# A hybrid attention block in split precision: halves of outputs summed by one VectorE reduction, MLP high parts squared by ScalarE

## The chip, the cores and the metric

The kernel runs on one core of one Trainium2 chip. The metric is the device time of one execution in microseconds (us); less is better.

## The reference, cut to what matters

Two layers of a transformer block on 512 tokens `x` and 256 context tokens `z` with width 1024. Each layer projects the tokens, runs three mixers beside each other (retention, neighbourhood attention, latent attention), merges them, and ends with a squared-ReLU MLP. In layer 1 the context is no longer carried on. All arithmetic is float32.

```python
def attend_blocks(q, k, v):
    ...
        s = jnp.einsum('bhqd,bhkd->bhqk', qi, k).astype(jnp.float32)
        p = jax.nn.softmax(s, axis=-1).astype(v.dtype)
        return jnp.einsum('bhqk,bhkv->bhqv', p, v)
def retention_chunkwise(q, k, v, log_gamma, s0):
    ...
    scores = jnp.einsum('bhncd,bhnsd->bhncs', qc, kc) * decay_mat[None, :, None]
    inner = jnp.einsum('bhncs,bhnsv->bhncv', scores, vc)
    kv_chunk = jnp.einsum('bhnsd,bhnsv->nbhdv', kc * k_decay[None, :, None, :, None], vc)
    ...
    cross = jnp.einsum('bhncd,nbhdv->bhncv', qc * q_decay[None, :, None, :, None], s_prev)
def sq_relu_mlp(h, p):
    return jnp.square(jax.nn.relu(h @ p['w_ff1'])) @ p['w_ff2']
```

## The kernel before

**Split precision.** TensorE multiplies in a rounded format (F32R). So that nothing is lost, each operand is kept as a pair: a high part, which ScalarE makes by copying the value into the rounded type (`hi_of`, the copy is at L381), and a low part, the value less its high part, which VectorE makes (`lo_of`, the subtraction at L384, on GpSimd for a few tiles). `split_into` calls both. A product of two pairs takes three passes (`mm3`): high with high (L428 or L643), high with low (L429, L644), low with high (L430, L645). Weights come from memory in tiles of 128x1024 (`wraw`) and are split in the same way into `wsp`.

**Halves.** In the attention's second product, values times probabilities, the value operand holds its high parts and its low parts side by side, 128 columns each. So an output bank holds two halves for every 256 columns, and their sum is the result. `gather_o` (L613 to L619) makes that sum for the neighbourhood and the latent attention: ScalarE copies one half out of the bank into a scratch tile `go` (L618), VectorE adds the other half from the bank (L619). It is called 80 times, on 512 columns each time. `Retention.prep` does the same for the chunks' key-value sums (L1292, L1293; 12 times), `Retention.item` in its step `s1` for its outputs `ro` (L1376, L1377; 40 times). Behind the sum of `s1` come the group norm's statistics, a power on GpSimd (L1386), and the gating. The retention's masked scores `pf` get their low part from GpSimd.

**Retention's preparation.** Behind the key-value sums, `prep` folds the chunk states (L1301), splits them into `st`, scales the queries into `qc` (L1319) and splits these into `op`; GpSimd casts copies of high parts (L665) and low parts (L666, the low part behind the high one).

**The MLP.** Eight blocks of 512 hidden columns, j = 0 to 7. For each, four weight tiles of the first matrix make four groups of hidden columns (i = 0 to 3): TensorE fills a bank, ScalarE applies Relu out of it into the scratch tile `rl` (L1751), VectorE squares `rl` in place (L1752), and the result is split into the operand `hid` (L381, L384). Then four weight tiles of the second matrix use these operands; the three first hidden groups are multiplied ahead, the fourth last. Blocks 1 to 6 handle all tokens in one round (512 columns of `x` and, in layer 0, 256 of `z`), blocks 0 and 7 go through the tokens in rounds of 256 columns. That makes 104 tiles `rl`, 56 with 512 columns and 48 with 256.

**Order.** The program is written stage by stage; the framework's scheduler arranges the instructions within each engine's queue, and each engine then works through its queue in order, waiting by semaphores for what the head of the queue needs. A few early loads are pinned to their written order. Memory for tiles comes from pools: 13 buffers of 128x512 (`sgl`, to which `go`, `rl`, `ro`, `qc` belong), 30 of 128x1024 (`dbl`), 3 of `wsp`. TensorE's banks: three for dense products (`pd`), two for the retention's and transposed products (`pst`), one for the attention outputs that gather_o empties (`pso`). An output bank is free again when the last of its readers is done.

Of the kernel before, what the change touches and what calls it, by code (L numbers as in the profile page):

```python
# [12 lines left out]
ALU = mybir.AluOpType  # L13
# [297 lines left out]
def block_kernel(ctx, tc, xT, zT, cond, wu, sp, bias, tab, out):  # L311
# [27 lines left out]
    def sgl(s="s"):  # L339
        return sgls.tile([128, 512], F32, tag="sgl", name=nm(s))  # L340
# [272 lines left out]

    def gather_o(t, o, nblk):

        v = o[:, : 256 * nblk].rearrange("p (b q) -> p b q", q=256)
        tmp = sgl("go")[:, : 128 * nblk].rearrange("p (b q) -> p b q", q=128)
        act.activation(tmp, v[:, :, 128:256], AF.Copy)  # L618
        dve.tensor_tensor(t, v[:, :, 0:128], tmp, op=ALU.add)  # L619

    def fold(y, t, odd):

# [528 lines left out]
    class Retention:  # L1151
# [39 lines left out]
        def prep(self, p2):  # L1191
# [89 lines left out]
            for c in range(3):  # L1281
                ps = bank_d()
                for o in range(2):
                    dst = ps[:, 256 * o : 256 * o + 256]
                    for i in range(2):
                        t = kt[2 * c + i]
                        v = R(vs[2 * c + i][:, 256 * o : 256 * o + 256])
                        pe.matmul(dst, R(t[:, 128 * o : 128 * o + 128]), v, start=i == 0, stop=False)
                        pe.matmul(dst, R(t[:, 256 + 128 * o : 256 + 128 * o + 128]), v, start=False, stop=i == 1)
                pv = ps.rearrange("p (h t v) -> p h t v", h=2, t=2)  # L1290
                s = kvt[c].rearrange("p (h v) -> p h v", h=2)
                act.activation(s, pv[:, :, 0], AF.Copy)  # L1292
                dve.tensor_tensor(s, pv[:, :, 1], s, op=ALU.add)  # L1293
                kvs.append(s)
                yield cost(8 * 256)

# [31 lines left out]
        def item(self, p2, o, c):  # L1328
# [25 lines left out]
            def s1():  # L1354
# [18 lines left out]
                            pe.matmul(ops[dr][:, ct], R(a), R(b), start=n == 0, stop=n == len(mms) - 1)  # L1373
                ov = st["ov"] = sgl("ro").rearrange("p (c t v) -> p c t v", c=2, t=2)
                for dr in range(2):
                    act.activation(ov[:, :, dr], ops[dr][:, :, 0], AF.Copy)  # L1376
                    dve.tensor_tensor(ov[:, :, dr], ops[dr][:, :, 1], ov[:, :, dr], op=ALU.add)  # L1377

                mv = small.tile([128, 4, 2], F32, tag="mv", name=nm("mv"))
                st6 = small.tile([128, 4, 6], F32, tag="st6", name=nm("st6"))  # L1380
# [240 lines left out]
    for l in range(DEPTH):  # L1621
# [119 lines left out]
        for j in range(8):  # L1741
            apart = j in (0, 7)
            for rnd in [[r] for r in rounds] if apart else [[(b, slice(0, n)) for b, (_, n) in enumerate(bufs)]]:
# [3 lines left out]
                for i in range(4):  # L1747
                    w = weight(l, "ff1", j, i)
                    for g, ps in enumerate(fm_groups(w, 0, hs, KT)):
                        t = sgl("rl")[:, : ns[g]]  # L1750
                        act.activation(t, ps, AF.Relu)  # L1751
                        dve.tensor_tensor(t, t, t, op=ALU.mult)  # L1752
                        split_into(hid[g][i], t)
                    later.step(0.0 if apart else ADA_MLP)
                    pend.step()
                last = j == 7
# [108 lines left out]
```

## Time and profile before

| | |
|---|---|
| time, median of 3 runs | 2628.12 us (2626.32 to 2634.21) |
| the profiled execution's own time | 2628.3 us |
| its span (first to last instruction) | 2626.5 us |
| mean granted clock of TensorE | 0.98 of full speed |
| TensorE busy (matmuls) | 2515.5 us, 96% of the span, 15218 instructions |
| VectorE busy | 1782.5 us, 68%, 3434 instructions |
| ScalarE busy | 1155.7 us, 44%, 2176 instructions |
| GpSimd busy | 333.4 us, 13%, 321 instructions |
| DMA | 329.43 MB moved, mean 125 GB/s |

A profile comes from one execution. PE is TensorE's matmul row, PEld its weight loads, DVE is VectorE, ACT ScalarE, POOL GpSimd; L619 is line 619 of the kernel. An instruction is written as engine, line, operation, tile written `<-` tiles read, size; a busy time is the sum over the instructions, and behind a bar stands how long the engine had stood idle before them and whose end it waited for. PEclk is the share of full clock that TensorE was granted.

### The profile page before, as it was taken

Reading aid. Unit: us, or ns where it says so; the run is one execution under the profiler, and the core shown is the slowest. Engines: PE = TensorE matmul, PEld = TensorE weight load, DVE = VectorE, ACT = ScalarE, POOL = GpSimd, SP = SyncE. Lnnn points to the kernel's source line nnn. Section 1 sums busy time; section 2 is a strip of 40 time slices with the busy share of each in tenths; the row PEclk is TensorE's granted clock in tenths of the full one; section 3 lists DMA queues with packets and bytes.
Section 4 is the critical chain, followed back from the end, with each engine's and each line's share of the span. In section 5 each row is a group of like instructions: output and inputs, shape, how many; then the busy total and the mean of one; then the engine's idle time right before and its main releaser. Section 6 shows DMA issues by size and latency. Waiting matters only on the chain. (4 is left out here: it accounts for less than half of the span.)

```text
span 2626.5 us, 39849 instructions
## 1 busy us (share of the span) xinstructions
PE 2515.5 (96%) x15218; PEld 2234.2 (85%) x15218; DVE 1782.5 (68%) x3434; ACT 1155.7 (44%) x2176; POOL 333.4 (13%) x321
## 2 busy tenths in 40 slices
PE   6999999998999998999999999999999899999997
PEld 4899998987888877888888878889888788988887
DVE  8566556777878886667556767665668768744457
ACT  4555545564333345322222446554555434732325
POOL 6201102234202000000000000010214310000000
PEclk7999999999999999999999999999999999999998
DMA  6222223423565633444444424323343356433333
GB/s 241 80 82 81 70 81 110 128 79 112 200 229 169 200 120 103 125 131 137 125 132 137 136 83 138 98 82 105 109 145 99 113 192 193 137 105 96 97 97 121
DMA packets 142995, 329.43 MB, mean 125 GB/s; under 512 B 16978, under 2 KB 54738, under 8 KB 142804
## 3 DMA queue, kind: packets, MB, share of 16 engines
q1 hardware_dynamic: 132436, 311.15, 38.6%
q10 hardware_dynamic: 10368, 15.73, 1.6%
q8 instruction: 120, 1.97, 0.3%
q14 instruction: 71, 0.58, 0.1%
HBM read 288.27 MB, written 36.45 MB: 124 GB/s over the span
## 5 line engine op out<-in xcount | busy, mean ns | idle before, releaser
L428 PE MATMUL pd<-op,wsp 128*128 128x512 f32 (+1 forms) x3080 | 1074.0, 350 | 29.1 <-ACT op L584 9.6
L429 PE MATMUL pd<-op,wsp 128*128 128x512 f32 (+1 forms) x3080 | 1071.9, 348 | 6.5 <-POOL op L384 4.9
L430 PE MATMUL pd<-op,wsp 128*128 128x512 f32 (+1 forms) x3080 | 1065.3, 347 | 11.6 <-DVE wsp L384 11.6
L428 PEld LDWEIGHTS pd<-op,wsp 128*128 128x128 f32 x3080 | 588.4, 191 | 104.7 <-ACT op L584 11.5
L430 PEld LDWEIGHTS pd<-op,wsp 128*128 128x128 f32 x3080 | 588.2, 191 | 83.9 <-DVE wsp L384 13.9
L429 PEld LDWEIGHTS pd<-op,wsp 128*128 128x128 f32 x3080 | 589.9, 192 | 78.0 <-POOL op L384 8.5
L381 ACT ACTIVATE wsp<-wraw 128x1024 fp32r<-128x1024 f32 x319 | 336.4, 1055 | 425.5 <-PE pd L430 295.0
L384 DVE TENSOR_TENSOR wsp<-wraw,wsp 128x1024 fp32r<-128x1024 f32 x319 | 392.0, 1232 | 190.6 <-ACT wsp L381 189.8
L643 PE MATMUL pd<-wsp,op 128*128 128x256 f32 x704 | 201.8, 287 | 2.1 <-DVE pr L753 1.6
L645 PE MATMUL pd<-wsp,op 128*128 128x256 f32 x704 | 200.5, 285 | 0.9 <-DVE wsp L384 0.9
L644 PE MATMUL pd<-wsp,op 128*128 128x256 f32 x704 | 200.2, 285 | 0.0
L1752 DVE TENSOR_TENSOR rl<-rl 128x256 f32<-128x256 f32 (+1 forms) x104 | 58.9, 567 | 149.8 <-ACT rl L1751 149.8
L384 DVE TENSOR_TENSOR pt<-pst,pt 128x512 fp32r<-128x512 f32 (+1 forms) x208 | 121.7, 604 | 47.1 <-ACT pt L381 45.3
L1522 POOL TENSOR_TENSOR tiny<-tiny,half 128x2 f32<-128x2 f32 (+1 forms) x8 | 9.0, 1128 | 1129.1 <-DVE tiny L1521 621.9
L1751 ACT ACTIVATE rl<-pd 128x256 f32<-128x256 f32 (+1 forms) x104 | 51.7, 498 | 226.3 <-PE pd L430 226.1
L1766 DVE TENSOR_TENSOR t<-pd,t 128x512 f32<-128x512 f32 (+1 forms) x132 | 80.9, 616 | 88.3 <-PE pd L430 87.9
L643 PEld LDWEIGHTS pd<-wsp,op 128*128 128x128 f32 x704 | 136.0, 193 | 3.2 <-issue 2.4
L645 PEld LDWEIGHTS pd<-wsp,op 128*128 128x128 f32 x704 | 135.8, 193 | 1.4 <-DVE wsp L384 1.4
L644 PEld LDWEIGHTS pd<-wsp,op 128*128 128x128 f32 x704 | 135.9, 193 | 0.1
L381 ACT ACTIVATE pt<-pst 128x512 fp32r<-128x512 f32 (+1 forms) x208 | 105.1, 529 | 51.7 <-PE pst L595 39.4
L612 PE MATMUL pso<-pt,t 128*128 128x256 f32 x704 | 114.7, 292 | 7.8 <-DVE ntx L619 2.4
L496 DVE CUSTOM_DVE_ANT_0 cond<-graw,cond,sp 128x1024 bf16<-128x1024 f32 x80 | 102.4, 1280 | 18.8 <-DMA graw<-wu 18.6
(280 smaller groups left out, 3667.4 us busy)
## 6 DMA issues: line engine op xcount, KB each, us to landing
wraw<-wu SPq DMA_DIRECT2D x327, 512.0 KB, 3.7
graw<-wu SPq DMA_DIRECT2D x56, 512.0 KB, 3.7
ada<-wu SPq DMA_DIRECT2D x40, 512.0 KB, 5.5
gg<-gate ACTq DMA_DIRECT2D x48, 256.0 KB, 2.0
gl<-gg SPq DMA_DIRECT2D x48, 256.0 KB, 3.3
zbias<-bias SPq DMA_DIRECT2D x64, 128.0 KB, 2.3
t<-vd SPq DMA_DIRECT2D x28, 256.0 KB, 5.3
gd<-gt SPq DMA_DIRECT2D x40, 128.0 KB, 2.2
```

The lines of the kernel that those rows point to most:

```text
L381: act.activation(R(dst), src, AF.Copy, scale=scale)
L384: (eng or dve).tensor_tensor(R(dst), src, hi, op=ALU.subtract)
L428: pe.matmul(ps, R(a[0]), R(b[0]), start=start, stop=False)
L429: pe.matmul(ps, R(a[0]), R(b[1]), start=False, stop=False)
L430: pe.matmul(ps, R(a[1]), R(b[0]), start=False, stop=stop)
L496: i = dve.tensor_tensor_reduce(cs[2], raw, cs[t], 0.5, spt[l][:, SP_BADA + c : SP_BADA + c + 1], ALU.mult, ALU.add, mods[l][:, c, t : t + 1])
L612: pe.matmul(o, R(vts[k]), R(pts[k]), start=k == 0, stop=k == n - 1)
L643: pe.matmul(ps, R(a[0]), R(w[0][:, o : o + 256]), start=k == 0, stop=False)
L644: pe.matmul(ps, R(a[1]), R(w[0][:, o : o + 256]), start=False, stop=False)
L645: pe.matmul(ps, R(a[0]), R(w[1][:, o : o + 256]), start=False, stop=k == nk - 1)
L1752: dve.tensor_tensor(t, t, t, op=ALU.mult)
L1766: dve.tensor_tensor(a, ps, a, op=ALU.add)
```

## The change

At the three places with halves, ScalarE's copy and VectorE's addition become one VectorE `tensor_reduce` that reads both halves from the bank and writes their sum: 80 times in `gather_o`, 12 in `Retention.prep`, 40 in `Retention.item`. The scratch tile `go` is gone. In the MLP, ScalarE computes the square of `rl` straight into the operand's high part (in the rounded type) in the place where it copied the squared value; VectorE still squares `rl` in place, exactly, and makes the low part from that exact square and the high part. Since ScalarE reads `rl` before it is squared, VectorE's square now waits for ScalarE's.

```diff
--- before.py
+++ after.py
@@ -613,10 +613,7 @@
 
     def gather_o(t, o, nblk):
 
-        v = o[:, : 256 * nblk].rearrange("p (b q) -> p b q", q=256)
-        tmp = sgl("go")[:, : 128 * nblk].rearrange("p (b q) -> p b q", q=128)
-        act.activation(tmp, v[:, :, 128:256], AF.Copy)
-        dve.tensor_tensor(t, v[:, :, 0:128], tmp, op=ALU.add)
+        dve.tensor_reduce(t, o[:, : 256 * nblk].rearrange("p (b t q) -> p b q t", t=2, q=128), AX, ALU.add)
 
     def fold(y, t, odd):
 
@@ -1289,8 +1286,7 @@
                         pe.matmul(dst, R(t[:, 256 + 128 * o : 256 + 128 * o + 128]), v, start=False, stop=i == 1)
                 pv = ps.rearrange("p (h t v) -> p h t v", h=2, t=2)
                 s = kvt[c].rearrange("p (h v) -> p h v", h=2)
-                act.activation(s, pv[:, :, 0], AF.Copy)
-                dve.tensor_tensor(s, pv[:, :, 1], s, op=ALU.add)
+                dve.tensor_reduce(s, pv.rearrange("p h t v -> p h v t"), AX, ALU.add)
                 kvs.append(s)
                 yield cost(8 * 256)
 
@@ -1373,8 +1369,7 @@
                             pe.matmul(ops[dr][:, ct], R(a), R(b), start=n == 0, stop=n == len(mms) - 1)
                 ov = st["ov"] = sgl("ro").rearrange("p (c t v) -> p c t v", c=2, t=2)
                 for dr in range(2):
-                    act.activation(ov[:, :, dr], ops[dr][:, :, 0], AF.Copy)
-                    dve.tensor_tensor(ov[:, :, dr], ops[dr][:, :, 1], ov[:, :, dr], op=ALU.add)
+                    dve.tensor_reduce(ov[:, :, dr], ops[dr].rearrange("p c h v -> p c v h"), AX, ALU.add)
 
                 mv = small.tile([128, 4, 2], F32, tag="mv", name=nm("mv"))
                 st6 = small.tile([128, 4, 6], F32, tag="st6", name=nm("st6"))
@@ -1749,8 +1744,10 @@
                     for g, ps in enumerate(fm_groups(w, 0, hs, KT)):
                         t = sgl("rl")[:, : ns[g]]
                         act.activation(t, ps, AF.Relu)
+
+                        act.activation(R(hid[g][i][0]), t, AF.Square)
                         dve.tensor_tensor(t, t, t, op=ALU.mult)
-                        split_into(hid[g][i], t)
+                        lo_of(hid[g][i][1], t, hid[g][i][0])
                     later.step(0.0 if apart else ADA_MLP)
                     pend.step()
                 last = j == 7
```

The scheduler puts the instructions in another order in some places. The names below are tiles with their running numbers, and a line number of the changed kernel is 3 to 5 lower than that of the kernel before.

**VectorE in the MLP of layer 1**, last hidden group but one and last of a block of 512 columns (`rl` the hidden tile, `op` the operand's low part, `wsp` a weight's low part). Before:

```order
L1752 TENSOR_TENSOR rl_23914<-rl_23914 128x512
L384 TENSOR_TENSOR wsp_23991<-wraw_23989,wsp_23991 128x1024
L384 TENSOR_TENSOR op_23810<-rl_23914,op_23810 128x512
L1752 TENSOR_TENSOR rl_23950<-rl_23950 128x512
L384 TENSOR_TENSOR wsp_24024<-wraw_24022,wsp_24024 128x1024
L384 TENSOR_TENSOR op_23811<-rl_23950,op_23811 128x512
```

And now:

```order
L1749 TENSOR_TENSOR rl_23702<-rl_23702 128x512
L384 TENSOR_TENSOR op_23598<-rl_23702,op_23598 128x512
L384 TENSOR_TENSOR wsp_23812<-wraw_23810,wsp_23812 128x1024
L1749 TENSOR_TENSOR rl_23738<-rl_23738 128x512
L384 TENSOR_TENSOR op_23599<-rl_23738,op_23599 128x512
```

The first square and the operand's low part now stand directly behind each other with the weight's low part after them; the second square comes right ahead of its low part, behind the weight.

**VectorE in the retention's preparation of layer 1** (`st` the states' low parts, `qc` the scaled queries, `op` their low parts, `wsp` a weight's low part). Before:

```order
L384 TENSOR_TENSOR st_21396<-t_21358,st_21396 64x2x128 x2
L384 TENSOR_TENSOR st_21397<-t_21358,st_21397 64x2x128 x2
L1319 TENSOR_TENSOR qc_21410<-ra_21074,qd_21041 64x512
L384 TENSOR_TENSOR op_21413<-qc_21410,op_21413 64x512
L1319 TENSOR_TENSOR qc_21418<-ra_21074,qd_21041 64x512
L384 TENSOR_TENSOR op_21413<-qc_21410,op_21413 64x512
L1319 TENSOR_TENSOR qc_21418<-ra_21074,qd_21041 64x512
L384 TENSOR_TENSOR op_21421<-qc_21418,op_21421 64x512
L1403 TENSOR_SCALAR ry_21462<-pso_21459,sp_95 128x256
L384 TENSOR_TENSOR wsp_21466<-wraw_21464,wsp_21466 128x1024
```

And now:

```order
L384 TENSOR_TENSOR st_21192<-t_21157,st_21192 64x2x128 x2
L384 TENSOR_TENSOR st_21193<-t_21157,st_21193 64x2x128 x2
L1315 TENSOR_TENSOR qc_21206<-ra_20879,qd_20846 64x512 x2
L1315 TENSOR_TENSOR qc_21214<-ra_20879,qd_20846 64x512 x2
L384 TENSOR_TENSOR op_21209<-qc_21206,op_21209 64x512 x2
L384 TENSOR_TENSOR op_21217<-qc_21214,op_21217 64x512 x2
L1398 TENSOR_SCALAR ry_21258<-pso_21255,sp_95 128x256
L384 TENSOR_TENSOR wsp_21262<-wraw_21260,wsp_21262 128x1024
L1398 TENSOR_SCALAR ry_21258<-pso_21293,sp_95 128x256
L384 TENSOR_TENSOR wsp_21300<-wraw_21298,wsp_21300 128x1024
```

All four pieces of `qc` and all four of `op` now stand together ahead of the first weight's low part. Before, three of each stood here; the first `qc` stood further up in the queue, and the last `op` behind the weight's low part.

**ScalarE at the same place** (high parts, by L381; `gate` is an activation that is then written to memory). Before:

```order
L381 ACTIVATE st_21396<-t_21358 64x2x128 x2
L381 ACTIVATE st_21397<-t_21358 64x2x128 x2
L381 ACTIVATE op_21413<-qc_21410 64x512
L1430 ACTIVATE gate_21456<-pd_21431 128x512
L381 ACTIVATE op_21413<-qc_21410 64x512
L1431 DMA gg_0_0_512_16892<-gate_21456 128x512
L381 ACTIVATE op_21421<-qc_21418 64x512
L381 ACTIVATE wsp_21537<-wraw_21535 128x1024
```

And now:

```order
L381 ACTIVATE st_21192<-t_21157 64x2x128 x2
L381 ACTIVATE st_21193<-t_21157 64x2x128 x2
L1425 ACTIVATE gate_21252<-pd_21227 128x512
L381 ACTIVATE wsp_21333<-wraw_21331 128x1024
L381 ACTIVATE op_21209<-qc_21206 64x512 x2
L381 ACTIVATE op_21217<-qc_21214 64x512 x2
L1426 DMA gg_0_0_512_16762<-gate_21252 128x512
```

The weight's high part (`wsp`) has moved ahead of the four pieces of the queries' high parts.

**GpSimd at the start of the retention's items in layer 0** (casts of 64x512, then the low parts of `pf`, then the power `rs`). Before:

```order
L665 CAST op_7394<-op_7394 64x256 x2
L666 CAST op_7395<-op_7395 64x256
L1221 TENSOR_TENSOR rb_7373<-rb_7373,rot_6993 128x512
L666 CAST op_7395<-op_7395 64x256
L665 CAST op_7382<-op_7382 64x512 x2
L666 CAST op_7383<-op_7383 64x512
L384 TENSOR_TENSOR pf_7415<-pf_7416,pf_7414 128x384
L666 CAST op_7383<-op_7383 64x512
L384 TENSOR_TENSOR pf_7415<-pf_7421,pf_7414 128x384
```

And now:

```order
L662 CAST op_7291<-op_7291 64x256 x2
L663 CAST op_7292<-op_7292 64x256 x2
L1218 TENSOR_TENSOR rb_7270<-rb_7270,rot_6894 128x512
L662 CAST op_7279<-op_7279 64x512 x2
L663 CAST op_7280<-op_7280 64x512 x2
L384 TENSOR_TENSOR pf_7312<-pf_7313,pf_7311 128x384
L384 TENSOR_TENSOR pf_7312<-pf_7318,pf_7311 128x384
```

The second cast of L666 (now L663) has moved from between the two low parts of `pf` to ahead of both, and the rotation tile `rb` now stands behind both casts of 64x256.

## Rows read from the trace of the kernel before

**Rows 1.** Busy by stretch, all engines: stretch, us, busy (instructions), PEclk, DMA, GB/s.

```profile
95.00:530.00 435.00, 431.83 (x2995) 398.16 (x2994) 275.86 (x568) 238.02 (x528) 56.80 (x67) 1.00 0.31 93
530.00:700.00 170.00, 148.38 (x999) 135.84 (x998) 129.42 (x314) 85.00 (x194) 69.00 (x72) 0.96 0.33 102
...
1950.00:2080.00 130.00, 114.58 (x762) 103.33 (x761) 105.47 (x244) 71.01 (x152) 53.58 (x54) 0.94 0.31 90
...
2270.00:2590.00 320.00, 319.96 (x1641) 274.63 (x1640) 168.25 (x218) 113.69 (x168) 0.45 (x1) 1.00 0.38 112
...
sum 2626.50, PE 2515.47 PEld 2234.20 DVE 1782.49 ACT 1155.65 POOL 333.37; mean PE 193.50 PEld 171.86 DVE 137.11 ACT 88.90 POOL 25.64
```

**Rows 2.** Waits of TensorE: who waits, for whom: us in total, times, longest.

```profile
PE pst L1373 <- DVE ro L1377: 7.0, 2, 6.5
...
PE pd L428 <- ACT op L381: 3.3, 4, 1.5
```

**Rows 3.** Line 619: who waited for it (us, times).

```profile
  PE pso L612: 6.8, 7
```

**Rows 4.** VectorE groups by form: busy, mean ns | idle before, releaser.

```profile
L1752 DVE TENSOR_TENSOR rl<-rl 128x256 f32<-128x256 f32 x48 | 20.2, 421 | 5.4 <-ACT rl L1751 5.4
...
L619 DVE TENSOR_TENSOR ntx<-pso,go 128x256 f32<-128x256 f32 x32 | 13.3, 416 | 0.3
...
L683 DVE TENSOR_REDUCE tiny<-pss 128x2 f32<-128x512 f32 x16 | 10.9, 682 | 6.2 <-PE pss L430 5.6 <-PE pss L671 0.6
```

**Rows 5.** ScalarE groups by form, the same view.

```profile
L381 ACT ACTIVATE op<-rl 128x512 fp32r<-128x512 f32 x56 | 34.9, 623 | 3.3 <-DVE rl L1752 3.3
...
L618 ACT ACTIVATE go<-pso 128x256 f32<-128x256 f32 x80 | 30.4, 380 | 3.8 <-PE pso L612 1.8 <-POOL ny L627 1.4
...
L1507 ACT ACTIVATE lnt<-t 128x512 f32<-128x512 f32 x14 | 8.7, 623 | 8.2 <-DVE t L1770 8.1
```

**Rows 6.** Busy by stretch, instructions of line 619 alone.

```profile
530.00:700.00 170.00, 4.58 (x11) 0.96 0.33 102
1950.00:2080.00 130.00, 2.90 (x7) 0.94 0.31 90
```

**Rows 7.** Busy by stretch, instructions of line 1377 alone.

```profile
530.00:700.00 170.00, 4.51 (x12) 0.96 0.33 102
1950.00:2080.00 130.00, 3.06 (x8) 0.94 0.31 90
```

**Rows 8.** Timeline at 600 us: start, us, engine, instruction [idle before <-releaser].

```profile
600.75 0.38 ACT L618 ACTIVATE go<-pso 128x256 f32<-128x256 f32 x1
...
603.34 0.42 DVE L619 TENSOR_TENSOR ntx<-pso,go 128x256 f32<-128x256 f32 x1
...
603.91 0.71 PE L612 MATMUL pso<-pt,t 128*128 128x256 f32 x4 [2.21 <-DVE ntx L619]
```

**Rows 9.** Busy in the 7 us after that stand, all engines.

```profile
657.00:664.00 7.00, 5.49 (x26) 5.52 (x27) 3.85 (x18) 0.94 (x3) 3.10 (x4) 0.51 0.02 6
```

**Rows 10.** Timeline of GpSimd at 656 us, layer 0's retention.

```profile
656.50 0.99 POOL L384 TENSOR_TENSOR pf<-pf,pf 128x384 fp32r<-128x384 f32 x1
```

**Rows 11.** Timeline of TensorE at 2076 us, layer 1's retention.

```profile
2075.74 0.80 PE L428 MATMUL pd<-op,wsp 128*128 128x512 f32 x1 [5.05 <-ACT wsp L381]
...
2077.81 0.79 PE L430 MATMUL pd<-op,wsp 128*128 128x512 f32 x1 [0.41 <-DVE wsp L384]
```

**Rows 12.** Timeline at 2319 us, MLP of layer 1.

```profile
2319.01 0.60 ACT L1751 ACTIVATE rl<-pd 128x512 f32<-128x512 f32 x1 [2.88 <-PE pd L430]
...
2319.64 0.69 DVE L1752 TENSOR_TENSOR rl<-rl 128x512 f32<-128x512 f32 x1 [2.67 <-ACT rl L1751]
...
2320.45 0.62 ACT L381 ACTIVATE op<-rl 128x512 fp32r<-128x512 f32 x1
...
2321.73 0.69 DVE L384 TENSOR_TENSOR op<-rl,op 128x512 fp32r<-128x512 f32 x1
...
2323.11 0.39 PE L429 MATMUL pd<-op,wsp 128*128 128x512 f32 x1
```

## Prediction

> **What bounds the kernel now.** I read the busy times first: TensorE is busy for 2515.5 us of the 2626.5 us span, VectorE for 1782.5 us (the sum line of [rows 1]). A change that touches ScalarE and VectorE alone can move the end only where TensorE stands still, some 111 us in all. The lines of the same table by stretch say where that is [rows 1]: from 95 to 530 us TensorE is busy 431.8 of 435 us, and from 2270 to 2590 us (the MLP of layer 1) 320.0 of 320; in 530 to 700 us (neighbourhood attention running into retention, layer 0) it is 148.4 of 170, with VectorE at 129.4, and in 1950 to 2080 us (the same place in layer 1) 114.6 of 130, with VectorE at 105.5. So the reader should look for an effect in these two stretches, 37 us of standing TensorE, and at the few block borders of the MLP. Then come TensorE's waits: for the attention output bank that gather_o empties 6.8 us in seven waits [rows 3], for the retention bank 7.0 us in two, and for a high part that ScalarE writes into an operand 3.3 us in four [rows 2].
>
> **The price of one reduction.** Each of the 132 places (80 in gather_o, 40 in Retention.item, 12 in Retention.prep) reads 128x512 elements from a bank and leaves 128x256. Before, ScalarE copies half of it in 0.380 us and VectorE adds the other half in 0.416 us [rows 4, 5]. The trace has no sum reduction of this form; the nearest row is the maximum over 128x512 from the same kind of bank, 0.682 us, though it writes two columns and not 256 [rows 4]. I take 0.682: a tensor_tensor that goes over 512 columns takes nearly that too, 0.69 for the square below, and it writes all 512 [rows 12]. The lower bound is the addition's own 0.416, the upper one reading and writing one after the other, 0.682 + 0.416 = 1.10 us. So VectorE gets 0.682 - 0.416 = 0.266 us more per place, 35 us in all, and ScalarE loses 132 x 0.380 = 50 us. The Trainium skill speaks against this swap: "VectorE: DVE Perf Modes", section "Rules for kernel authors", calls tensor_reduce the slowest VectorE operation, to be restructured away on a hot path. If every place were hot the sum would be 2628.3 + 35 = 2663; the rows say that most are not. In the two stretches lie 11 + 7 of gather_o's [rows 6], 12 + 8 of the retention item's [rows 7] and, by the code, all 12 of the prep's: 50. The other 82 I cost at nothing: TensorE's own matmuls cover them, as from 95 to 530 us, where it stands 3.2 of 435 us [rows 1]; without that cover they would cost up to 22 us.
>
> **Where a reduction is on the path.** The wait that the change shortens (ScalarE's copy, then a hand-over) is mostly not the one that ends last. At 603.9 us TensorE has stood 2.21 us for the bank; ScalarE's copy began at 600.75 and was long done, but VectorE came to the addition only at 603.34, behind the qc and op work of the retention prep [rows 8]. In the new order the reduction has the same place in VectorE's queue, so this wait grows by 0.266 us instead of shrinking. The three longest waits for that bank in 530 to 610 us grow so (3 x 0.27), and two of the prep's reductions stand ahead of the longest (2 x 0.27): +1.35 us.
>
> The 6.5 us stand before 658.5 us: the ro tile's buffer comes free when GpSimd has done the low part of pf, at 656.50 + 0.99 [rows 10]; the reduction waits for GpSimd as the copy did. In GpSimd's new order one more 64x512 cast (0.61 us) goes ahead of that low part, and copy + addition (0.38 + 0.42) become 0.68: +0.55 us. That stand is followed by a granted clock of 0.51, the lower of TensorE's two levels (1.2 of 2.4 GHz), for the next 7 us [rows 9]; I count no more of that, because the stand exists on both sides.
>
> At 2077.8 us in layer 1 VectorE is the chain: TensorE stands 0.41 us there for a weight's low part, after 5.05 us for another weight's high part [rows 11]. Ahead of that low part now stand seven reductions; one of the adds moved into a wait for GpSimd, another hides in one, which leaves about four: +1.0 us, and one more qc and op pair is put before the low part, while it waits less for ScalarE: +0.3. The high part comes earlier (its conversion now precedes ScalarE's four op pieces), but the matmul behind it needs the low part anyway, so nothing is gained. Four smaller stands of TensorE behind VectorE in the two stretches get 0.27 us each: +1.1. Sum of this part: 1.35 + 0.55 + 1.3 + 1.1 = 4.3 us.
>
> **The MLP.** The Square takes ScalarE the time of the copy that it replaces (0.623 against 0.623 us [rows 5]), and no VectorE instruction goes away. But the exact square is written in place, over the tile that the Square reads, so it has to wait for the Square; "beside" is not what the queues do. At 2319 us the chain was Relu (2319.01), exact square (2319.64), a weight's low part, the operand's low part (2321.73, done 2322.42); TensorE wants that low part at 2323.11 [rows 12]. Now the weight's low part comes first, then the square, then the operand's low part, which is done about 0.6 us later, at 2323.0: TensorE still gets it in time, by 0.1 us. The high part comes when it did, since the weight's conversion stands between Relu and Square as before. Cost for the 128x512 blocks: nothing. In the six blocks with 256 columns alone (first and last j) the cover is half as long and the low part 0.34 us later (a square of 0.421 us [rows 4], less its overlap): five of them cost 0.34, and in the first one ScalarE's new order has the Square right behind the Relu, which brings the wait for the high part down by some 0.6: 5 x 0.34 - 0.6 = +1.1 us.
>
> **The sum** is made against the profiled execution, 2628.3 us (span 2626.5 and 1.8 around it), which is 0.2 above the median of the three runs: 2628.3 + 4.3 + 1.1 = **2633.7 us**, 0.2% more than before. A measurement of this kernel tells about 0.3% (7.9 us) from no change, so this is no change.
>
> **The rivals.** *Hand-overs decide (faster).* If the copy's hand-over, or ScalarE's queue blocked behind it, is what ends the waits, all 6.8 us for the output bank and the 3.3 us for high parts go [rows 2, 3], and with them one stretch of lower clock, 7 us at half rate, 3.4 us [rows 9]: 2628.3 - 13.5 = 2614.8. For it: ScalarE's queue loses 50 us of work, and its head stood waiting for banks. Against: the addition that came last for its own queue, 2.6 us after the copy began [rows 8]. Chance 0.14.
>
> *VectorE's queue passes everything on (slower).* If VectorE is the bound throughout the two stretches, all 50 x 0.266 = 13.3 us arrive at TensorE, and a longer stand brings one more stretch at the lower clock, 3.4 us: 2645. It decides once VectorE has no idle time left between two stands of TensorE; at 129.4 of 170 and 105.5 of 130 us it is near that in pieces, not throughout [rows 1]. Chance 0.25.
>
> *The reduction is dearer (slower).* At the upper bound of 1.10 us, 0.68 more than the addition, the same 50 places give 34 us: 2662. Against: the square goes over 512 columns in and out in 0.69 [rows 12]. Chance 0.10. The skill's rule named above stands behind this rival and the one before it.
>
> *The Square doesn't run beside the exact square* is no rival but part of the forecast; if the low parts came later still, it would show at all 20 block ends: at 0.3 us each, 6 us, which is inside the range.
>
> **How the numbers follow.** The forecast has 0.51, of which 0.03 lies over the bound: its own range is 2627 to 2638 (the chain terms nought or doubled). Faster by over 0.3% (under 2620.2): 0.14. Within: 0.48. Slower (over 2636.0): 0.25 + 0.10 + 0.03 = 0.38. The range of 8 in 10 leaves out the dearer reduction and half of the edge of either other rival: 2617 to 2647 us.
>
> **What would show it.** Right: TENSOR_REDUCE rows of 128x256 from 128x512 at 0.65 to 0.72 us; VectorE 1782 up to about 1818 us, ScalarE down to about 1105; the wait for the bank at some 604 us not shorter; in the MLP the exact square starting after ScalarE's Square, the operand's low part ending 0.6 us later, and TensorE still without a gap from 2270 to 2590 us; TensorE's stand in 530 to 700 and 1950 to 2080 us longer by 3 to 5 us together. Wrong: a reduction far from 0.68 us; waits for the output bank that nearly vanish; a stand before 658 us that goes, and the lower clock after it too; new waits of TensorE for low parts in the middle of the MLP; or a granted clock that falls in a place where it was full.

## The result and the profile after

The changed kernel takes 2647.7 us (median of 4 runs, 2647.65 to 2650.31) against 2627.74 for the kernel before in the same series: a ratio of 1.0075, 95% interval 1.0063 to 1.0088, that is 16.6 to 23.1 us slower. The prediction was 2633.7 with a range that ended at 2647.0, so the time lies just outside it, and what was forecast as no change is a loss. Below, a ratio's "us" is the ratio less 1 times 2628.

Busy times of the changed kernel, from its page (span 2645.9 us):

```profile
PE 2527.5 (96%) x15218; PEld 2238.7 (85%) x15218; DVE 1820.9 (69%) x3434; ACT 1117.3 (42%) x2044; POOL 333.8 (13%) x321
```

VectorE's 1820.9 us are 38.4 more than before, ScalarE's 1117.3 are 38.4 less. The span is 19.4 us longer: TensorE's standing time grew from 111.0 to 118.4 us (span less busy time), and its busy time by 12.0 us for the same 15218 matmuls. Part of the latter is the clock: a mean of 0.980 over 2626.5 us before and of 0.978 over 2645.9 after, so 52.5 and 58.2 us of full rate not granted, some 5 us more.

The price of the new instructions, groups by form (columns as in [rows 4]):

```profile
L1749 DVE TENSOR_TENSOR rl<-rl 128x512 f32<-128x512 f32 x56 | 38.3, 684 | 0.0
...
L1748 ACT ACTIVATE op<-rl 128x512 fp32r<-128x512 f32 x56 | 34.9, 623 | 0.0
...
L1372 DVE TENSOR_REDUCE ro<-pst 128x256 f32<-128x512 f32 x40 | 26.3, 682 | 6.9 <-PE pst L1369 4.5 <-POOL pf L384 2.3
```

A reduction takes 0.682 us here (0.678 in `prep`, 0.682 to 0.684 in gather_o), the 0.682 that was taken from the maximum [rows 4]. ScalarE's Square takes 0.623 us, what the copy took [rows 5]. VectorE's square of 512 columns has no idle time ahead of it any more: it is called when ScalarE's Square is done, behind other work.

Where the time went shows in the view of single lines, of which the first and the last start are milestones (columns: line, engine, operation, tiles, count, shortest/median/longest ns, first and last start). Before, gather_o's sums, the MLP's Relu and the retention's last step:

```profile
L619 DVE TENSOR_TENSOR ntx<-pso,go x32: 399/415/426, 431.1 to 2005.9; 128x256 f32<-128x256 f32 x32
...
L1751 ACT ACTIVATE rl<-pd x104: 360/597/599, 980.9 to 2595.6; 128x512 f32<-128x512 f32 x56, 128x256 f32<-128x256 f32 x48
...
L1403 DVE TENSOR_SCALAR ry<-pso,sp x20: 443/476/485, 659.6 to 2173.1; 128x256 f32<-128x256 f32 x20
```

And after:

```profile
L616 DVE TENSOR_REDUCE ntx<-pso x32: 666/683/692, 431.2 to 2018.4; 128x256 f32<-128x512 f32 x32
...
L1746 ACT ACTIVATE rl<-pd x104: 358/597/600, 994.9 to 2615.1; 128x512 f32<-128x512 f32 x56, 128x256 f32<-128x256 f32 x48
...
L1398 DVE TENSOR_SCALAR ry<-pso,sp x20: 446/466/485, 661.4 to 2193.0; 128x256 f32<-128x256 f32 x20
```

The attention of layer 0 ends (its last sum, `tz`, in the same view) at 608.7 and 610.7 us: 2.0 later. The MLP of layer 0 starts (first `rl`) at 980.9 and 994.9: 14.0 later. The attention of layer 1 ends (last `ntx`) 12.5 later, the retention of layer 1 (last `ry`) 19.9, the last Relu 19.5. So 12 us are lost between 609 and 981 us, some 7 in the retention of layer 1, and between the first and the last Relu of the MLP of layer 1 next to nothing.

The table of busy times says the same from TensorE's side. The changed kernel (columns as in [rows 1]):

```profile
530.00:700.00 170.00, 147.82 (x958) 133.82 (x958) 133.72 (x315) 74.90 (x160) 67.79 (x72) 0.92 0.32 100
700.00:950.00 250.00, 240.95 (x1439) 213.24 (x1439) 205.57 (x422) 70.82 (x115) 21.88 (x18) 0.99 0.63 199
...
2080.00:2270.00 190.00, 179.78 (x1028) 157.25 (x1027) 147.55 (x301) 74.70 (x114) 20.78 (x18) 0.96 0.55 175
2290.00:2610.00 320.00, 320.00 (x1627) 272.74 (x1627) 167.17 (x216) 113.52 (x169) 0.02 (x1) 1.00 0.38 111
```

Beside 530 to 700 and 2270 to 2590 in [rows 1], two stretches of the kernel before that the prediction did not read:

```profile
700.00:950.00 250.00, 244.61 (x1468) 217.46 (x1467) 210.99 (x453) 79.16 (x134) 23.23 (x19) 1.00 0.63 203
...
2080.00:2270.00 190.00, 184.37 (x1096) 163.90 (x1096) 143.99 (x309) 82.54 (x134) 16.82 (x14) 0.98 0.56 177
```

From 530 to 700 us TensorE gets 958 matmuls done where it did 999, at a clock of 0.92 instead of 0.96, and from 700 to 950 us 1439 instead of 1468. In the first the standing time hardly grew: 170 us less 148.38 and less 147.82 busy, so 21.6 and 22.2 us. The clock explains the missing matmuls: 999 x 0.92 / 0.96 = 957. In the second of these VectorE was busy 211.0 of 250 us before: this is where the later items of the retention lie. The middle of the MLP of layer 1 (here shifted by 20 us) is without a gap that the page shows, 320.00 of 320; that it still lost time shows further down.

TensorE's waits in the changed kernel (columns as in [rows 2]):

```profile
PE pso L1393 <- DVE ry L1398: 11.8, 3, 6.2
...
PE pd L428 <- DVE ms L1483: 4.9, 8, 1.4
...
PE pst L1369 <- DVE ro L1372: 3.6, 3, 2.2
...
PE pso L612 <- DVE ntx L616: 2.2, 1, 2.2
```

The two of before that the first two of these answer to:

```profile
PE pso L1398 <- DVE ry L1403: 2.4, 2, 1.6
...
PE pd L428 <- DVE ms L1488: 1.9, 3, 0.8
```

The wait for gather_o's bank at 604 us is what was forecast, not shorter (2.2 us in one wait). The new wait is another: TensorE's transposes of a retention item (L1393, L1398 before) stand for VectorE's `ry`, 11.8 us where it was 2.4, and matmuls stand for `ms`, the merge's product that empties a bank, 4.9 instead of 1.9. The longest of the waits for `ry`, 6.2 us in layer 1, comes with `prep`'s reductions: ret_only below has it too (11.5 us in all, longest 6.2), item_only has not (4.9, longest 3.8). The timeline around the wait for `ry` in layer 0, columns as in [rows 8]:

```profile
689.90 0.69 DVE L384 TENSOR_TENSOR op<-qc,op 64x512 fp32r<-64x512 f32 x1
...
690.62 0.69 DVE L1372 TENSOR_REDUCE ro<-pst 128x256 f32<-128x512 f32 x1
691.34 0.69 DVE L384 TENSOR_TENSOR op<-qc,op 64x512 fp32r<-64x512 f32 x1
691.95 0.68 DVE L1372 TENSOR_REDUCE ro<-pst 128x256 f32<-128x512 f32 x1
...
693.66 0.45 DVE L1398 TENSOR_SCALAR ry<-pso,sp 128x256 f32<-128x256 f32 x1
...
694.17 0.69 PE L1393 MATMUL pso<-ctab,ro 128*128 128x128 f32 x2 [4.70 <-DVE ry L1398]
```

TensorE has the transposes at the head of its queue from 689.5 us on. They need the one output bank, which `ry` empties, and `ry` stands in VectorE's queue behind two low parts, two reductions (0.69 and 0.68 us) and the group norm's statistics. In the kernel before, the same transposes stood 18 places later in TensorE's queue, and it stood only 1.61 us for them, at 691.9 us. From 693.6 to 700.2 us the granted clock is 0.50.

### The profile page after: what moved, and what is told of

It reads as the page before. It is cut to its first block, busy times and chain, and to the rows that moved or that the text cites. A ratio compares the mean times of both kernels' runs of the same rounds, so it can differ in the third digit from the quotient of the medians.

```text
span 2645.9 us, 39741 instructions
## 1 busy us (share of the span) xinstructions
PE 2527.5 (96%) x15218; PEld 2238.7 (85%) x15218; DVE 1820.9 (69%) x3434; ACT 1117.3 (42%) x2044; POOL 333.8 (13%) x321
## 4 chain that ended last, share of the span: by engine, by line
PE 58%; DVE 9%; issue 3%; ACT 2%; POOL 1%; DMA 1%; SPq 0%; POOLq 0%; ACTq 0%; DVEq 0%
PE pd L430 16%; PE pd L428 16%; PE pd L429 16%; PE pso L612 1%; PE pst L595 1%; PE pd L640 1%; PE pd L642 1%; PE pd L641 1%; DVE wsp L384 1%; DVE op L384 1%; ACT wsp L381 1%; POOL rs L1381 1%; DVE ro L1384 1%; DVE cond L496 1%; POOL pf L384 0%
## 5 line engine op out<-in xcount | busy, mean ns | idle before, releaser
L381 ACT ACTIVATE wsp<-wraw 128x1024 fp32r<-128x1024 f32 x319 | 336.3, 1055 | 434.6 <-PE pd L430 359.7
L381 ACT ACTIVATE pt<-pst 128x512 fp32r<-128x512 f32 (+1 forms) x208 | 105.0, 528 | 55.3 <-PE pst L595 43.5
L496 DVE CUSTOM_DVE_ANT_0 cond<-graw,cond,sp 128x1024 bf16<-128x1024 f32 x80 | 102.4, 1279 | 23.8 <-DMA graw<-wu 23.6
L1425 ACT ACTIVATE gate<-pd 128x512 f32<-128x512 f32 x72 | 37.8, 525 | 176.9 <-PE pd L430 176.6
```

The costliest lines, as they stand in the source:

```text
L381: act.activation(R(dst), src, AF.Copy, scale=scale)
L496: i = dve.tensor_tensor_reduce(cs[2], raw, cs[t], 0.5, spt[l][:, SP_BADA + c : SP_BADA + c + 1], ALU.mult, ALU.add, mods[l][:, c, t : t + 1])
```

## The experiments

Theories: **1**, VectorE's price is passed on to TensorE where VectorE sets the pace, and that is the retention; **2**, the scheduler makes another order of the queues, and the order costs; **3**, ScalarE's saved copies bring something. The expectations name differences of medians; the table gives ratios, which compare with the kernel before in the same series of runs and are what the text uses.

| kernel | ratio | 95% interval | us |
|---|---|---|---|
| gather_only | 0.9988 | 0.9979 to 0.9997 | -3.2 |
| gather_held | 1.0034 | 1.0021 to 1.0046 | +8.9 |
| ret_only | 1.0045 | 1.0032 to 1.0058 | +11.8 |
| item_only | 1.0038 | 1.0025 to 1.0050 | +10.0 |
| item_peorder | 1.0038 | 1.0025 to 1.0050 | +10.0 |
| before_peorder | 1.0029 | 1.0020 to 1.0037 | +7.6 |
| dose_held | 1.0056 | 1.0043 to 1.0068 | +14.7 |
| prep_held | 1.0015 | 1.0005 to 1.0026 | +3.9 |
| mlp_only | 1.0027 | 1.0018 to 1.0036 | +7.1 |
| mlp_held | 1.0095 | 1.0079 to 1.0110 | +25.0 |
| mlp_ft | 0.9998 | 0.9989 to 1.0007 | -0.5 |
| mlp_ft_held | 1.0002 | 0.9992 to 1.0011 | +0.5 |
| after_peorder | 1.0071 | 1.0059 to 1.0084 | +18.7 |
| after_ft | 1.0037 | 1.0025 to 1.0049 | +9.7 |
| gather_ft | 0.9971 | 0.9960 to 0.9982 | -7.6 |

### One part at a time

Each takes one part of the diff above into the kernel before: gather_only the edit of `gather_o`, ret_only the two of `prep` and `item`, mlp_only that of the MLP, item_only that of `item`.

gather_only. 

> The 80 reductions of gather_o alone; retention and MLP as before. Theory 1 (VectorE's price is passed on where VectorE is the bound, which is the retention): gather_o's places are covered by TensorE's matmuls, so -2 to +3 us against the kernel before. Theory 2 (the new order of the queues is what costs, wherever it comes from): +4 to +10 us, since TensorE's order moves around here too. Theory 3 (ScalarE's saved copies are worth something where TensorE waits for the output bank): -5 to -10 us.

ret_only. 

> The 52 reductions of the retention (12 in prep, 40 in the items) alone. Theory 1: nearly the whole loss is here, +14 to +20 us: 52 x 0.266 = 13.8 us of VectorE time, 20 of the reductions in the later items that the prediction had costed at nothing, plus one or two more stretches of lower clock. Theory 2: a part of it only, +4 to +10 us, and the three parts do not add up to the whole.

mlp_only. 

> ScalarE's Square in the MLP alone. The prediction's own sum says +1.1 us for it, with theory 1 the same: -1 to +3 us. Theory 2: several us, of either sign, by order alone.

item_only. 

> The 40 reductions of the retention's items alone, without the prep's 12. Theory 1: 40 of the 52, 40 x 0.266 = 10.6 us and a stretch of lower clock: +9 to +16 us. If the prep's 12 carry the loss (they stand ahead of the queries' split that the later stage waits for), +0 to +6 us.

The retention carries the most: +11.8, of it +10.0 in the items. gather_o's 80 reductions, which are most of VectorE's added time, make the kernel 3.2 us faster, and the MLP's Square, forecast at +1.1, costs 7.1. The three parts add up to 15.7 us, against 19.7 for the whole; with intervals of 2 to 3.5 us to either side of each, that is no proof of more than their sum. No theory had all of it: 1 said nothing for the MLP and at least 14 us for the retention, 2 expected gather_o to lose and at most 10 us for the retention.

### The same with TensorE's queue, or every queue, in the old order

A few lines after the program is written add edges of order (no waits) between neighbours of a queue, by a recorded list:

```diff
+def hold_order(tc, nc, engine, packed):
...
+    place = np.cumsum(step)
+    rows = [i for i in nc.cur_bb.bb.instructions if i.engine == engine and i.opcode not in UNHELD]
...
+    for a, b in zip(place, place[1:]):
+        tc.add_manual_dep(rows[b], rows[a].name, mybir.DependencyInfo(mybir.DependencyClass.NoSync, mybir.DependencyReason.DATA), reason="order")
...
+        hold_order(tc, nc, mybir.EngineType.PE, PE_ORDER)
```

In "peorder" kernels TensorE's queue alone is held, in "held" kernels all five. TensorE's order differs in 371 of 15128 places between item_only and before, and in 1232 between the whole change and before.

item_peorder. 

> The 40 reductions of the items, with TensorE's queue held in the order that it has in the kernel before (the other queues as the scheduler makes them). Measured without the hold: +8.2 us. Theory 1 (price: each reduction makes VectorE's queue 0.266 us later, and TensorE waits for that): +7 to +10 us again. Theory 2 (order: the scheduler puts TensorE's transposes of an item some 18 matmuls earlier, so that TensorE stands at the head of its queue while matmuls that could run are behind): -2 to +3 us.

before_peorder. 

> The kernel before, without any reduction, with TensorE's queue held in the order that it has in the kernel with the 40 reductions of the items. Theory 1: the order is worth nothing without the price, 0 to +2 us. Theory 2: the order alone carries the loss, +6 to +11 us.

after_peorder. 

> The whole change with TensorE's queue held in the order of the kernel before. Measured without the hold: +19.6 us. Theory 1: +15 to +20 us. Theory 2: 0 to +9 us, what is left being the orders of the other queues and the price at the places where VectorE is the bound.

Both theories are partly right. With TensorE's old order the items' reductions still cost 10.0 us, so the price is real, and it is paid elsewhere: waits of TensorE in item_peorder:

```profile
PE pd L428 <- DVE ms L1487: 4.3, 5, 1.8
...
PE pso L1397 <- DVE ro L1390: 3.0, 1, 3.0
```

Nearly all of the wait for `ms` (1.9 us before) lies at 849 to 893 us, the longest one for `ro` at 2180 us: behind the later items, which the prediction had costed at nothing. But the new order costs too when nothing else is changed: before_peorder has no reduction in place of a sum and is 7.6 us slower. It loses at the place of the changed kernel's new stand (busy times as in [rows 1], from 650 to 710 us, of before_peorder and then of the kernel before):

```profile
650.00:710.00 60.00, 49.50 (x286) 43.99 (x285) 50.42 (x134) 19.26 (x40) 18.14 (x19) 0.89 0.46 153
```

```profile
650.00:710.00 60.00, 49.09 (x297) 44.04 (x296) 50.31 (x135) 20.60 (x42) 20.23 (x22) 0.94 0.44 147
```

286 matmuls at a clock of 0.89 against 297 at 0.94. (The profiled execution is the fastest of its eleven runs, 2631.8 us, and shows only part of the 7.6.)

So the two do not add: 10.0 for the price in the old order, 7.6 for the order without the price, 10.0 for both together (item_only). For the whole change the old order of TensorE brings 1 us of 19.7, which is less than the noise.

dose_held. The kernel before, every queue held, and one more instruction behind each sum of an item:

```diff
                     dve.tensor_tensor(ov[:, :, dr], ops[dr][:, :, 1], ov[:, :, dr], op=ALU.add)
+                    dve.tensor_scalar(ov[:, :, dr, :32], ov[:, :, dr, :32], 1.0, 0.0, op0=ALU.mult, op1=ALU.add)
```

> The kernel before with every queue in its own order, and behind each of the 40 sums of the items one more VectorE instruction (a multiplication by 1 over 128x64, by the nearest rows about 0.27 to 0.3 us): the reductions' price and nothing else, ScalarE's copies stay. If the price alone is passed on to TensorE (theory 1): +7 to +12 us, as with the 40 reductions under TensorE's old order (+9.9). If the loss there came from the lost copies or from the other queues' new orders: 0 to +3 us.

The added line (columns as in [rows 4]), two of its instructions with what GpSimd did beside the first, and TensorE's waits:

```profile
L1378 DVE TENSOR_SCALAR ro<-ro 128x64 f32<-128x64 f32 x40 | 15.2, 379 | 1.4
```

```profile
659.46 1.00 POOL L384 TENSOR_TENSOR pf<-pf,pf 128x384 fp32r<-128x384 f32 x1
659.62 0.89 DVE L1378 TENSOR_SCALAR ro<-ro 128x64 f32<-128x64 f32 x1
...
660.87 0.20 DVE L1378 TENSOR_SCALAR ro<-ro 128x64 f32<-128x64 f32 x1
```

```profile
PE pso L1399 <- DVE ry L1404: 4.9, 3, 2.0
...
PE pd L428 <- DVE ms L1489: 3.6, 3, 2.4
```

This is the cleanest of them: nothing but VectorE time is added, though it also makes the way from the bank to `ry` longer, which a reduction doesn't. And the dose came out larger than planned. Where GpSimd has nothing running, a sum and the new instruction hold the queue for 0.56 us by the starts in the timeline, where the sum alone held it for 0.33 (the reduction holds it for 0.60). That would be 40 x 0.23 = 9.2 us. 24 of the 40 new instructions took 0.19 to 0.20 us so; the other 16, each beside a GpSimd instruction, took 0.27 to 1.11 us. VectorE's busy time grew by 14.2 us (1796.7 against 1782.5), and the kernel's time by 14.7 us, above the range of theory 1. So VectorE's time is passed on about in full. TensorE waits longer for `ry` and `ms` (4.9 and 3.6 us; before 2.4 and 1.9); its standing time grew by 9.5 us, its busy time by 5.0, with a mean clock of 0.978 over 2641.0 us, 58.1 us of full rate not granted against 52.5. Compared matmul by matmul (the n-th of one trace with the n-th of the other), it is 5.3 us late at 700 us and 10.4 us late at 890 us: the later items of layer 0, which the prediction had costed at nothing, make half of that. With the 40 reductions, 40 x 0.266 = 10.6 us of VectorE time made 10.0 (item_peorder). Theory 1 is shown for the items.

prep_held. 

> The 12 reductions of prep alone, every queue in the order of the kernel before. Theory 1 with the prediction's account (they stand ahead of the queries' split in both layers, where TensorE waits): 12 x 0.266 = 3.2 us at most, +1 to +4 us. If they are covered: -1 to +1 us.

+3.9 us for 12 reductions with 3.2 us of VectorE time between them: passed on in full, as the rival of the prediction had it; the interval, 1.3 to 6.8 us, allows half as well.

gather_held. 

> The 80 reductions of gather_o with every queue in the order of the kernel before (ScalarE's without its copies). Without the hold: -3.3 us. If VectorE's price is passed on at the 18 places of the two stretches: +1 to +5 us. If they are covered and ScalarE's saved copies bring nothing: -1 to +1 us. If the saved copies bring the gain: -3 to -7 us.

+8.9 us, 42% of 80 x 0.266 = 21.3 us, more than any theory had, and 12 us worse than the same instructions in the scheduler's order. TensorE's waits in gather_held:

```profile
PE pso L612 <- DVE ntx L616: 5.3, 7, 2.7
...
PE pso L612 <- DVE tx L616: 3.5, 5, 1.1
...
PE pso L612 <- DVE tz L616: 1.7, 3, 1.0
```

and in gather_only:

```profile
PE pso L612 <- DVE ntx L616: 2.3, 1, 2.3
...
PE pso L612 <- DVE tz L616: 0.4, 1, 0.4
```

Before, TensorE waited seven times for the bank, 6.8 us in all [rows 3]. In the old order the dearer sum comes late fifteen times (5.3, 3.5 and 1.7 us); in the scheduler's new order twice (2.3 and 0.4 us), and in the whole change twice too. At three places of layer 1's latent attention the price arrives whole: stands of 0.85, 1.07 and 1.07 us (1644, 1675 and 1704 us) where there were 0.58, 0.81 and 0.81. So the saved copies by themselves are not what gives gather_only its gain: in the old order they are saved too. The scheduler's new order hides the price there, and does not in the retention.

### The MLP's Square

mlp_held. 

> ScalarE's Square in the MLP with every queue held in the order of the kernel before. Measured without the hold: +5.4 us. If the Square that the exact square waits for costs the time: +4 to +6 us again. If the new order costs it (VectorE's conversions of the next layer's conditioning weights, which wait for a load, come ahead of the sums that empty TensorE's banks at 1104 us, and other work at the start): -1 to +2 us.

mlp_ft_held and mlp_ft. Against the changed MLP, the exact square goes into a tile of a pool (`ft`) that the MLP does not use:

```diff
                         act.activation(R(hid[g][i][0]), t, AF.Square)
-                        dve.tensor_tensor(t, t, t, op=ALU.mult)
-                        lo_of(hid[g][i][1], t, hid[g][i][0])
+                        t2 = ft("sq")[:, : ns[g]]
+                        dve.tensor_tensor(t2, t, t, op=ALU.mult)
+                        lo_of(hid[g][i][1], t2, hid[g][i][0])
```

mlp_ft_held. 

> ScalarE's Square in the MLP, but the exact square goes into a tile of its own (of a pool that the MLP does not use otherwise), so that VectorE does not wait for ScalarE; every queue in the order of the kernel before. The same with the square in place: +25 us. If the wait for the Square is the cause: -4 to +2 us. If the Square itself, or reading the Relu's result from two engines, is slow: +10 to +25 us.

mlp_ft. 

> The same without the hold. With the square in place the scheduler's order gave +5.4 us. If that was the wait and the order made to avoid it: -4 to +2 us. If the scheduler's order is bad by itself: +3 to +8 us.

In one and the same order, the square in place costs 25.0 us, far above both ranges, and the square into another tile 0.5, which is nothing: it is the wait for ScalarE's Square and neither the Square nor its reading. VectorE's exact squares of 512 columns, in mlp_held and in the kernel before (columns as in [rows 4]):

```profile
L1754 DVE TENSOR_TENSOR rl<-rl 128x512 f32<-128x512 f32 x56 | 38.8, 693 | 185.8 <-ACT op L1753 185.8
```

```profile
L1752 DVE TENSOR_TENSOR rl<-rl 128x512 f32<-128x512 f32 x56 | 38.7, 692 | 144.3 <-ACT rl L1751 144.3
```

VectorE stands longer, and for the Square where it stood for the Relu. That the own tile lets `rl` go earlier plays no part: ScalarE's Relu waits for nothing but TensorE in both. TensorE's waits for operands in mlp_held:

```profile
PE pd L429 <- DVE op L384: 10.4, 16, 1.6
```

and in mlp_ft_held:

```profile
PE pd L429 <- DVE op L384: 1.6, 3, 1.2
```

10.4 us in 16 waits for a low part, against 1.6 in three: 0.31 us in each of the middle blocks of layer 1, more at the first and the last block of a layer. The last Relu starts 22.6 us later than before, 13 of them lost after the last `ry`. Part of the rest is the clock (0.978 over 2651.4 us, 0.981 over 2627.7). The scheduler's new order evades most of it, with 7.1 us left in mlp_only. How, shows in the changed kernel (timeline, MLP of layer 1):

```profile
2339.69 1.23 DVE L384 TENSOR_TENSOR wsp<-wraw,wsp 128x1024 fp32r<-128x1024 f32 x1 [2.88 <-ACT wsp L381]
...
2340.84 0.68 DVE L1749 TENSOR_TENSOR rl<-rl 128x512 f32<-128x512 f32 x1
...
2341.55 0.69 DVE L384 TENSOR_TENSOR op<-rl,op 128x512 fp32r<-128x512 f32 x1
...
2341.99 0.39 PE L428 MATMUL pd<-op,wsp 128*128 128x512 f32 x1
...
2342.30 0.50 PE L429 MATMUL pd<-op,wsp 128*128 128x512 f32 x1
...
2342.64 0.40 PE L430 MATMUL pd<-op,wsp 128*128 128x512 f32 x1
```

and in the kernel before, around the matmul of [rows 12]:

```profile
2322.89 0.39 PE L428 MATMUL pd<-op,wsp 128*128 128x512 f32 x1
...
2323.34 0.39 PE L430 MATMUL pd<-op,wsp 128*128 128x512 f32 x1
```

Weight's low part, exact square, operand's low part, which ends at 2342.24; TensorE takes it at 2342.30. The prediction had "TensorE still gets it in time, by 0.1 us". It is late instead: the matmuls start 0.31 and 0.34 us after one another where it was 0.22 and 0.23, so 0.2 us are lost, and the busy times don't show it, since the matmul before is counted as running until then. Matmul by matmul, this happens in each of the six middle blocks of layer 1. Their stretch (2300 to 2570 us before, the 13672nd to the 14909th matmul) takes 271.10 us in the changed kernel and in mlp_only, 269.82 before and in mlp_ft_held and mlp_ft.

The other and larger loss of mlp_only lies in the middle of layer 0's MLP (1035 to 1470 us before, the 6177th to the 8674th matmul: 435.06 us before and in mlp_ft, 439.24 in mlp_only), at one place, with the busy times behind it (columns as in [rows 1]):

```profile
1102.89 1.28 DVE L496 CUSTOM_DVE_ANT_0 cond<-graw,cond,sp 128x1024 bf16<-128x1024 f32 x1 [2.03 <-DMA graw<-wu]
...
1106.37 0.76 PE L428 MATMUL pd<-op,wsp 128*128 128x512 f32 x1 [2.11 <-DVE t L1768]
```

```profile
1106.50:1115.00 8.50, 8.50 (x37) 7.09 (x38) 5.88 (x11) 0.00 (x0) 0.00 (x0) 0.80 0.56 152
```

Here the new order puts conversions of conditioning weights, the first of which waits for its load, ahead of the sums `t` that empty TensorE's banks. That is the rival that the expectation of mlp_held named. The stand of 2.1 us and 8.5 us at a clock of 0.80 (1.7 us of full rate) make 3.8 of the 5.9 us by which this execution's span is longer. In the changed kernel the stand at this place is 0.76 us.

### The whole without the MLP's wait, and a version that beats both

after_ft. The whole change with the MLP's edit of mlp_ft.

> The whole change, but with the exact square of the MLP in a tile of its own, queues as the scheduler makes them. The whole change is +19.6 us; its parts alone were -3.3 (gather_o), +11.2 (retention) and +5.4 (MLP), together 13.3. If the parts add up: the MLP's 5.4 go and leave +6 to +10 us. If the excess of 6 us over the sum belongs to the MLP's wait too: the same or less, +2 to +8 us. If it belongs to the new orders of the queues between gather_o and retention: +11 to +16 us.

+9.7 us, as if the parts added up: half of the loss of 19.7 goes with the MLP's wait and the order made around it. What is left is about the retention's 11.8 less gather_o's 3.2.

gather_ft. gather_o's reductions and the MLP's edit of mlp_ft, the retention as before.

> gather_o's reductions and the MLP's Square with the exact square in a tile of its own, the retention as before; queues as the scheduler makes them. If both parts keep what they bring alone: -3 to -7 us, faster than both kernels. If the gain of gather_o alone was the luck of an order: -2 to +4 us.

```profile
PE 2513.2 (96%) x15218; PEld 2233.0 (85%) x15218; DVE 1806.3 (69%) x3434; ACT 1135.5 (43%) x2096; POOL 338.2 (13%) x321
```

2621.0 us (median of 7 runs), 7.6 us faster than the kernel before and some 27 faster than the changed one, although VectorE is busy 23.8 us more than before. That the ratio of gather_only (0.9988) and that of mlp_ft (0.9998) give only part of the 0.9971 was not followed up; the intervals are wide enough for the sum to be all of it.

## Why the prediction was wrong

**The price was right.** 0.682 us for a reduction, 0.623 for the Square, VectorE up by 38 us (35 was said). ScalarE went down by 38 instead of 50.

**What failed first is the cover.** "The other 82 I cost at nothing: TensorE's own matmuls cover them." That sentence had read one stretch, 95 to 530 us, for all 82. Twenty of them are the later items, at 790 to 855 and 2125 to 2165 us, in stretches where VectorE was busy 211.0 of 250 and 144.0 of 190 us; neither stretch was read. dose_held and item_peorder show what VectorE time costs there: half of the 10.4 us that dose_held has lost by 890 us. And even gather_o's covered places let 42% through when the order stays (gather_held).

**What failed second is that the order was held to be the old one but for three places.** "In the new order the reduction has the same place in VectorE's queue" was true at 604 us, and there the wait came out not shorter: 2.2 us (the wait for `ntx` above), before 2.21 [rows 8]; the 0.27 us added do not show. But that the 6.5 us stand before 658.5 us "exists on both sides" was wrong: the scheduler moved 24 of TensorE's matmuls ahead of it, it is down to 2.2 us (the wait for `ro` above), and behind it come stands of 1.3, 3.0 and 4.7 us where there were 2.1 and 1.6. The prediction looked at the orders of VectorE, ScalarE and GpSimd and never at TensorE's, the engine that bounds. (Its term for that stand is also added wrongly: 0.61 + 0.68 - 0.38 - 0.42 is 0.49, not 0.55.)

**What failed third is the clock, a term put at nothing.** "I count no more of that, because the stand exists on both sides." From 530 to 700 us TensorE's standing time grew by 0.6 us, less than was forecast, but the granted clock fell from 0.96 to 0.92: 6.8 us of full rate over 170 us, and so nearly all of the 41 missing matmuls. That is the prediction's own sign of being wrong, "a granted clock that falls in a place where it was full": 0.50 from 693.6 to 700.2 us, where it was 1.00 before.

**At 2077 us** the weight's high part did come earlier, as said: 0.86 us of standing where it was 5.05 [rows 11]. Right behind it stands a wait of 6.23 us for `ry`, which no term had.

**The MLP** was right in mechanism (the square in place waits) and too small: +1.1 against 7.1 in mlp_only, and 10 between the whole and after_ft. The term that failed is "Cost for the 128x512 blocks: nothing." The middle blocks take 2.7 us more in the changed kernel (436.52 against 435.06 us in layer 0, 271.10 against 269.82 in layer 1), and 5.5 us more in mlp_only; with the square in a tile of its own they take what they took before. In layer 1 it is the late low part, in layer 0 mostly the new order of VectorE's queue, which no term had. The first and last blocks, for which the prediction had its +1.1, take 0.4 us more in the changed kernel (203.5 against 203.1 us, all four together).

**The rivals.** "VectorE's queue passes everything on" (2645 us, chance 0.25) is what came nearest, 2.7 us off, with the retention's 40 + 12 places about in full and gather_o's not, and with more time at the lower clock. That its number is so near is partly luck: the MLP's loss, which it lacks, stands in for gather_o's places, which it has. "Hand-overs decide" is refuted as a mechanism: gather_held saves 80 copies and is slower. The rule of the Trainium skill behind the slower rivals ("VectorE: DVE Perf Modes", section "Rules for kernel authors": tensor_reduce is the slowest operation, consider restructuring on a hot path) agrees with the retention's +11.8 us; in gather_o the same instruction came with a gain, and over 512 columns it took no longer (0.682 us) than the square of as many (0.684).

**Still open.** The items with reductions were not tried with every queue held, only with TensorE's. Why the scheduler's order hides the price in gather_o and not in the retention is not shown. Of the 10 us between the whole and after_ft, the middle blocks are 2.7; the rest is not assigned.

## What to carry to other kernels

Before work at a place is called covered, read the bound engine's and the second engine's busy time in that very stretch, for every stretch where the edit occurs, not for one. Where a scheduler sets the order, compare the order of the engine that bounds first, and test an edit twice, in the new order and with the old one held: the same instructions were worth -3 or +9 us here, and +25 or +7. Two engines ran side by side on one tile only where the one that writes had a tile of its own to write to (0.5 us against 25.0 in one order). And a busy share of 100% can hide lost time: compare the starts of the same matmuls too.

## What the runs showed that was not expected

A sum reduction that writes 256 columns costs VectorE the same 0.68 us as a maximum over the same 128x512 that writes two. A small VectorE instruction (128x64, a multiplication by 1) took 0.19 to 0.20 us in 24 of 40 places, and 0.27 to 1.11 us in the 16 where GpSimd ran an instruction beside it (dose_held). And 371 of 15128 places of TensorE's queue in another order, with nothing else changed, cost 7.6 us.
